# A decoder layer with routed experts: w_out's columns permuted in the split, the residual stored once, x's tile given to expert weights

## The chip, the cores and the metric

The kernel runs on one core of a Trainium2 chip. The metric is device time in microseconds (us), the median of three runs; lower is better.

## The reference, cut to what matters

```
h   = rms_norm(x, norm_attn)                       # x: 256 tokens x 1024
P   = h @ w_in                                     # queries, latent, dilated q/k/v, two gates
A   = latent attention;  Bd = dilated attention in three groups, merged
merged = sigmoid(gA) * (A @ w_o_mla) + sigmoid(gB) * (Bd @ w_o_dil)
x   = x + merged @ w_out                           # 1024 x 1024
h2  = rms_norm(x, norm_ffn)
gp  = softmax(h2 @ w_rg + b_rg); one of 4 groups per token
ep  = softmax of the 8 experts' logits of that group; the best two, renormalised
y   = sum over a token's experts of  weight * (silu(h2 @ w_gate[e]) * (h2 @ w_up[e])) @ w_down[e]
out = x + y                                        # 32 experts, d_ff 256
```

All tensors are f32. The experts' weights are 96 MiB of the 144 MB that are read from memory.

## The kernel before

Tokens stand in two blocks of 128 (tb 0 and 1), one token per partition. Every matmul of the first part (w_in to w_out) is done in three passes of a rounded format: each weight is split into a high part (ScalarE: a rounding copy, tile wh) and a low part (weight minus high part, tile wl, mostly on GpSimd in two operations of 128x512, now and then on VectorE), and each half unit, two blocks of 128 rows and 512 columns, takes 12 matmuls. wh and wl have three buffers each, so a split waits until TensorE has used the half unit three ahead of it. Raw weights come through four slots of 1 MiB (ring), loaded by SyncE's queue; a slot is loaded again when its last split has been read.

What order the instructions have is decided when the program is built, by a small simulator in the kernel (Weave) with prices for each engine; each engine then runs its queue in order.

w_out is the last matrix of the first part: Chunk objects outs[0] and outs[1] are its two column halves, and add_half lists eight half units. The last two are run block by block, each followed by x_out(tb, half): VectorE adds the residual in x1 to the accumulator and writes x1 back, and the squares are summed for the norm (ScalarE, for the last one VectorE). x_turn transposes the new x on TensorE for the router, logits multiplies by the router's weights, out_rms computes the reciprocal root in nine tiny steps (generator rms0 on GpSimd, rms1 on VectorE), and route picks groups and experts on VectorE; its two blocks' steps are interleaved. The experts' matmuls run on gathered tokens: gather multiplies tok (x with columns sorted by k of q*8 + k) by a one-hot matrix of 32 slots for each expert. x_sorted makes tok from x1, three times on GpSimd and once on ScalarE. warm_up issues matmuls without a use, to keep TensorE busy while VectorE routes.

The experts are done in eight groups g of four. Each group needs twelve loads of 1 MiB in order (four w_gate, four w_up, four w_down). All slots that the first part no longer needs (side, late_slot, oT, hT0, ring, and xs0 to xs3, which lie on the first part's buffers) become slots for expert weights: release(slot) puts a slot in the queue of free ones and pump issues the next loads of moe_loads on SyncE. There are 23 such slots with the four early ones, and a group's slots are given back after its gate, its up and its down matmuls. Group 0's gate slots (early) are loaded again in halves. In group 0 four matmuls with the identity put the residual x1 into the banks ys, to which combine adds each group's result. The last group's result is copied into x1 and stored.

Of the kernel before, what the change touches and what calls it, by code (L numbers as in the profile page):

```python
# [22 lines left out]
P = 128  # L23
# [36 lines left out]
TUNE = dict(gap=0.103, dV=0.05, dS=0.208, dG=0.121, dPE=0.257, early=-0.366, norm=0.02, split1=-0.463, split2=1.641, pace=2.246, small=9.132, masks=18.02, busy=6, first=40.0, space=0.0, busy2=0, busy3=4, rms=4.0, angles=3.0, keep=2, keep2=2, keep3=6, route=7, route2=6)  # L60
# [82 lines left out]
def layer(ctx, tc, A, out):  # L143
# [93 lines left out]
    with ExitStack() as c1:  # L237
# [42 lines left out]
        R_CKV, R_GQ, R_GK, R_MQ, R_MK, R_FFN = 0, 2, 5, 8, 9, 10  # L280
# [712 lines left out]
        def x_out(tb, half):  # L993

            xs, acc = x1[:, tb, half * 512:(half + 1) * 512], sso[:, tb, half:half + 1]
            V.scalar_tensor_tensor(xs, outs[half].acc[tb], 0.5, xs, op0=ALU.mult, op1=ALU.add)
            if tb and half:
                V.tensor_tensor_reduce(out=sqs[1], in0=xs, in1=xs, scale=1.0 / D, scalar=0.0, op0=ALU.mult, op1=ALU.add,
                                       accum_out=acc)
            else:  # L1000
                S.activation(sqs[0], xs, AF.Square, scale=D ** -0.5, accum_out=acc)

        def x_sorted(tb, half, E):
            src = x1[:, tb, half * 512:(half + 1) * 512].rearrange("p (q k) -> p k q", k=8)
            dst = tok[:, tb, :, half * 64:(half + 1) * 64]
            if E is S:
                S.activation(dst, src, AF.Copy)
            else:
                E.tensor_copy(dst, src)

        def x_turn(tb, half):
            for k in range(4):
                PE.transpose(pts[half][:, k], x1[:, tb, half * 512 + k * P:half * 512 + (k + 1) * P], ident)
            dst = xT[tb][:, 4 * half:4 * half + 4]
            S.copy(dst, pts[half])
# [76 lines left out]

        outs = [Chunk(A["w_out"][0], hTh, hTl, 8, 512, None, wait_merged(0)) for half in range(2)]
        out_u = {(k0, half): add_unit(outs[half].w, k0, 4, half * 512, 512) for k0 in (0, 4) for half in range(2)}
        for k0, q, half in ((0, 0, 0), (0, 2, 0), (0, 0, 1), (0, 2, 1), (4, 0, 0), (4, 0, 1), (4, 2, 0), (4, 2, 1)):
            add_half(outs[half], out_u[k0, half], q, 0, k0 + q)
# [17 lines left out]
        SP.dma_start(rows[R_FFN:R_FFN + 8], A["norm_ffn"].rearrange("o (k p) -> (o k) p", p=P))  # L1114
# [4 lines left out]
        def split_src(i):  # L1119
            hv = halves[i]  # L1120
            n = hv["c"].n
            return [hv["u"]["t"][:, hv["q"]:hv["q"] + 2, hv["col"]:hv["col"] + n]] + \
                [t[i % NSPLIT][:, :2 * n].rearrange("p (k n) -> p k n", k=2) for t in (whs, wls)]
# [207 lines left out]
        def router_weights():  # L1331
            yield 120.0
            SP.dma_start(rbias[:, NE:], bcast(A["b_router_group"], EG))
            SP.dma_start(rbias[:, :NE], bcast(A["b_router_expert"], NE))
            SP.dma_start(wr[:, :, NE:], A["w_router_group"].rearrange("o (k p) n -> p (o k) n", p=P))
            SP.dma_start(wr[:, :, :NE], A["w_router_expert"].rearrange("o (k p) n -> p (o k) n", p=P))
            SP.dma_start(g8, A["norm_ffn"].rearrange("o (q k) -> q (o k)", k=8))
            yield 30.0
            for k in range(8):
                G.tensor_scalar(wr[:, k], wr[:, k], cols[:, R_FFN + k:R_FFN + k + 1], None, op0=ALU.mult)  # L1340
                yield 2.0
# [10 lines left out]
        def half_unit(i, tbs=(0, 1)):  # L1352
# [15 lines left out]
            hi, lo, ready = split_of[i]  # L1368
            weave.ready, weave.last = ready, None
# [32 lines left out]
        for half in range(2):  # L1402
            x_sorted(0, half, G)
        half_unit(n_last + 1, (1,))
        x_out(1, 1)
        x_turn(1, 0)
        logits(0, 0)
        x_turn(1, 1)
        x_sorted(1, 0, G)
        x_sorted(1, 1, S)  # L1410
# [7 lines left out]
        rms1, r0, r1 = out_rms(1, V), route(0), route(1)  # L1418
# [27 lines left out]
    with ExitStack() as c2:  # L1446
# [136 lines left out]
        ov = out.rearrange("b (t p) d -> p (b t) d", p=P)  # L1583
        for g in range(NGRP):
# [43 lines left out]
            if g == 0:  # L1628
                for tb in range(2):
                    for half in range(2):  # L1630
                        PE.matmul(ys[2 * tb + half], ident, x1[:, tb, half * 512:(half + 1) * 512], start=True,
                                  stop=False, skip_group_check=True)

            def combine(piece):
# [3 lines left out]
                for tb in range(2):  # L1638
                    PE.matmul(yv[tb], trs[:, 2 + tb], dos[piece], start=False, stop=final, skip_group_check=True)
                if final:  # L1640
                    sl = slice(c0, c0 + n)
                    S.activation(x1[:, 0, sl], yv[0], AF.Copy)
                    V.tensor_copy(x1[:, 1, sl], yv[1])
                    nc.scalar.dma_start(ov[:, 0, sl], x1[:, 0, sl])
                    SP.dma_start(ov[:, 1, sl], x1[:, 1, sl])
# [54 lines left out]
```

## Time and profile before

| what | value |
|---|---|
| median of three runs | 514.99 us (514.86 to 515.1) |
| the profiled execution | 515.22 us |
| its span, first to last instruction | 513.4 us |
| TensorE busy | 463.3 us (90%) |
| GpSimd busy | 236.7 us (46%) |
| VectorE busy | 215.1 us (42%) |
| ScalarE busy | 170.2 us (33%) |
| read from memory | 144.00 MB |

The span is one execution as the hardware profiler recorded it; the time has 1.8 us more around it. In the profile's rows PE is TensorE, PEld its weight loads, DVE VectorE, ACT ScalarE, POOL GpSimd and SP SyncE; SPq is SyncE's queue of load commands. Almost every compute instruction has line L128, that of a recording helper, so rows are told apart by the names of tiles: x is x1, pj an accumulator, s and pt banks, gu, pd, px, tr and y the banks of the experts' part.

### The profile page before, as it was taken

How to read it: one execution, taken by the hardware profiler on the slowest of the kernel's cores; microseconds unless marked ns; L12 is line 12 of the kernel's file. 1: busy time of each engine (PE TensorE's matmuls, PEld its weight loads, DVE VectorE, ACT ScalarE, POOL GpSimd, SP SyncE). 2: the span in 40 equal slices, each digit the busy share in tenths (PEclk: the TensorE clock that was granted, in tenths of full speed). 3: DMA queues.
4: the chain of work that ended last, by engine and by line, in shares of the span. 5: the costliest groups of instructions: out<-in, count | busy, mean ns of one | idle time of the engine just before them, and what ended most of it. 6: DMA issues, size and time to landing. Idle time of an engine off the chain costs nothing.

```text
span 513.4 us, 8417 instructions
## 1 busy us (share of the span) xinstructions
PE 463.3 (90%) x3280; PEld 328.9 (64%) x3280; DVE 215.1 (42%) x516; ACT 170.2 (33%) x326; POOL 236.7 (46%) x266
## 2 busy tenths in 40 slices
PE   7939889998999999999999999997988878768997
PEld 4839668887778888888888886462535444325343
DVE  5985796648853430483344166122212130202002
ACT  4417546665654664475445330000000000000001
POOL 5828779786877889368698740000000000000000
PEclk9979999999999999999999999999999999988999
DMA  8653776655434545359896986999999999999992
GB/s 286 216 168 104 281 285 194 201 165 164 97 95 152 165 153 179 101 157 373 314 363 233 423 335 252 423 420 421 419 420 421 418 419 423 420 419 421 410 345 92
DMA packets 43956, 145.63 MB, mean 284 GB/s; under 512 B 5752, under 2 KB 11402, under 8 KB 33162
## 3 DMA queue, kind: packets, MB, share of 16 engines
q1 hardware_dynamic: 43194, 144.53, 74.6%
q8 instruction: 27, 0.44, 0.4%
q10 hardware_dynamic: 720, 0.53, 0.3%
q14 instruction: 15, 0.12, 0.1%
HBM read 144.00 MB, written 1.05 MB: 283 GB/s over the span
## 4 chain that ended last, share of the span: by engine, by line
PE 56%; DMA 26%; DVE 6%; POOL 6%; issue 4%; ACT 1%; SPq 0%; POOLq 0%; DVEq 0%; ACTq 0%
PE pj L128 36%; DMA xs<-in_w_up_dram 8%; PE pt L128 6%; DMA side<-in_w_gate_dram 4%; DMA side<-in_w_up_dram 4%; DMA oT<-in_w_down_dram 4%; PE gu L128 3%; POOL wl L128 3%; PE px L128 3%; PE s L128 3%; DMA ring<-in_w_down_dram 3%; PE y L128 3%; DMA early<-in_w_down_dram 2%; PE pd L128 2%; DMA ring<-in_w_in_dram 1%
## 5 line engine op out<-in xcount | busy, mean ns | idle before, releaser
L128 PE MATMUL pj<-wh,hT 128*128 128x512 f32 (+2 forms) x576 | 192.7, 397 | 3.3 <-DVE late_slot L128 1.8
L128 POOL TENSOR_TENSOR wl<-ring,wh 128x512 fp32r<-128x512 f32 (+2 forms) x130 | 162.7, 1276 | 53.3 <-ACT wh L128 52.7
L128 PEld LDWEIGHTS pj<-wh,hT 128*128 128x128 f32 x576 | 111.2, 195 | 24.0 <-ACT wh L128 3.8
L128 PE MATMUL pj<-wl,hT 128*128 128x512 f32 (+2 forms) x288 | 111.2, 386 | 0.7 <-DVE wl L128 0.7
L128 ACT ACTIVATE wh<-ring 128x1024 fp32r<-128x1024 f32 (+2 forms) x78 | 79.4, 1018 | 83.7 <-PE pj L128 66.1
L128 POOL TENSOR_TENSOR wc<-wc,comb 128x128 f32<-128x128 f32 x16 | 6.0, 399 | 171.1 <-DVE wc L128 171.1
L128 PEld LDWEIGHTS pj<-wl,hT 128*128 128x128 f32 x288 | 56.4, 196 | 8.1 <-DVE wl L128 0.9
L128 PE MATMUL gu<-side,xg 128*32 128x256 f32 x416 | 44.1, 401 | 5.4 <-DMA side<-in_w_up_dram 4.6
L128 ACT ACTIVATE he<-gu 128x256 f32<-128x256 f32 x8 | 3.1, 383 | 127.2 <-PE gu L128 127.2
L128 PE MATMUL y<-do,trs 128*128 128x512 f32 x56 | 27.8, 618 | 11.7 <-DVE do L128 6.6
L128 DVE SCALAR_TENSOR_TENSOR he<-he,gu 128x256 f32<-128x256 f32 x8 | 3.4, 421 | 82.6 <-ACT he L128 82.6
L128 POOL TENSOR_TENSOR side<-side,st 128x512 f32<-128x512 f32 (+2 forms) x32 | 30.8, 990 | 5.9 <-DVE st L128 5.9
L128 PEld LDWEIGHTS gu<-side,xg 128*32 128x32 f32 x416 | 21.1, 116 | 16.7 <-DMA side<-in_w_up_dram 6.5
L128 PEld LDWEIGHTS y<-do,trs 128*128 128x128 f32 x56 | 9.5, 189 | 31.1 <-DVE do L128 12.9
L128 DVE COPY do<-px 128x512 f32<-128x512 f32 x7 | 4.8, 691 | 50.3 <-PE px L128 50.3
L128 PE MATMUL gu<-ring,xg 128*32 128x256 f32 x176 | 25.7, 380 | 0.0
L128 DVE COPY side<-pt 128x512 f32<-128x512 f32 (+2 forms) x26 | 16.6, 645 | 17.4 <-PE pt L128 16.1
L128 DVE TENSOR_TENSOR wl<-ring,wh 128x1024 fp32r<-128x1024 f32 (+1 forms) x13 | 17.1, 1316 | 15.2 <-ACT wh L128 15.1
L128 PE MATMUL pt<-ident,late_slot 128*128 128x128 f32 (+1 forms) x84 | 13.2, 281 | 11.0 <-DVE cols L128 7.8
L128 ACT ACTIVATE do<-pd 128x512 f32<-128x512 f32 x7 | 4.2, 597 | 52.3 <-PE pd L128 52.3
L128 PE MATMUL pj<-wh,oT 128*128 128x512 f32 x64 | 21.1, 398 | 0.0
L128 PE MATMUL gu<-xs,xg 128*32 128x256 f32 x160 | 19.0, 381 | 2.1 <-DMA xs<-in_w_up_dram 2.1
(274 smaller groups left out, 753.7 us busy)
## 6 DMA issues: line engine op xcount, KB each, us to landing
ring<-in_w_in_dram SPq DMA_DIRECT2D x25, 1024.0 KB, 5.2
side<-in_w_up_dram SPq DMA_DIRECT2D x16, 1024.0 KB, 17.6
side<-in_w_gate_dram SPq DMA_DIRECT2D x10, 1024.0 KB, 18.5
early<-in_w_gate_dram SPq DMA_DIRECT2D x7, 1024.0 KB
side<-in_w_down_dram SPq DMA_DIRECT2D x6, 1024.0 KB, 5.0
ring<-in_w_gate_dram SPq DMA_DIRECT2D x6, 1024.0 KB, 17.0
xs<-in_w_up_dram SPq DMA_DIRECT2D x6, 1024.0 KB
xs<-in_w_down_dram SPq DMA_DIRECT2D x6, 1024.0 KB, 18.6
```

The source lines that it names most:

```text
L128: r = f(*args, **kw)
```

## The change

x_out now adds the residual and writes straight into tok, in the gathers' order. For that the accumulators must come in that order, so w_out's columns are permuted when its splits are made: split_src reads a slot as 8 columns apart ("p k (q r) -> p k r q"), and a unit is two row blocks of all 1024 columns in place of four of 512, since half r0 to r0+3 takes columns from everywhere. x_out reads x1 with the same step. x_sorted and its four calls go. x_turn reads tok, and the router's weights are loaded with rows in that order (and scaled by g8, a tile that was there already, so one small load of norm_ffn goes). x1 is released as a slot for expert weights after the last x_out: 24 slots. The residual enters the banks in group 2, read from tok with a step of 128, and group 0's combine starts them. The result is stored from tok. rms1 runs on GpSimd. In TUNE, route goes from 7 to 3 and route2 from 6 to 4 (the numbers of warm-up matmuls).

```diff
         def x_out(tb, half):
-            xs, acc = x1[:, tb, half * 512:(half + 1) * 512], sso[:, tb, half:half + 1]
-            V.scalar_tensor_tensor(xs, outs[half].acc[tb], 0.5, xs, op0=ALU.mult, op1=ALU.add)
+            rs = slice(4 * half, 4 * half + 4)
+            xs, acc = tok[:, tb, rs], sso[:, tb, half:half + 1]
+            V.scalar_tensor_tensor(xs, outs[half].acc[tb].rearrange("p (r q) -> p r q", r=4), 0.5,
+                                   x1[:, tb].rearrange("p (q r) -> p r q", r=8)[:, rs], op0=ALU.mult, op1=ALU.add)
+            xs = xs.rearrange("p r q -> p (r q)")
...
-        def x_sorted(tb, half, E):
-            src = x1[:, tb, half * 512:(half + 1) * 512].rearrange("p (q k) -> p k q", k=8)
-            dst = tok[:, tb, :, half * 64:(half + 1) * 64]
-            if E is S:
-                S.activation(dst, src, AF.Copy)
-            else:
-                E.tensor_copy(dst, src)
-
         def x_turn(tb, half):
             for k in range(4):
-                PE.transpose(pts[half][:, k], x1[:, tb, half * 512 + k * P:half * 512 + (k + 1) * P], ident)
+                PE.transpose(pts[half][:, k], tok[:, tb, 4 * half + k], ident)
...
-        out_u = {(k0, half): add_unit(outs[half].w, k0, 4, half * 512, 512) for k0 in (0, 4) for half in range(2)}
-        for k0, q, half in ((0, 0, 0), (0, 2, 0), (0, 0, 1), (0, 2, 1), (4, 0, 0), (4, 0, 1), (4, 2, 0), (4, 2, 1)):
-            add_half(outs[half], out_u[k0, half], q, 0, k0 + q)
+        out_u = [add_unit(outs[0].w, k0, 2, 0, D) for k0 in range(0, 8, 2)]
+        for i, half in ((0, 0), (1, 0), (0, 1), (1, 1), (2, 0), (2, 1), (3, 0), (3, 1)):
+            add_half(outs[half], out_u[i], 0, half, 2 * i)
...
-            return [hv["u"]["t"][:, hv["q"]:hv["q"] + 2, hv["col"]:hv["col"] + n]] + \
-                [t[i % NSPLIT][:, :2 * n].rearrange("p (k n) -> p k n", k=2) for t in (whs, wls)]
+            parts = [t[i % NSPLIT][:, :2 * n].rearrange("p (k n) -> p k n", k=2) for t in (whs, wls)]
+            if hv["c"] in outs:
+                r0 = 4 * hv["col"]
+                return [hv["u"]["t"].rearrange("p k (q r) -> p k r q", r=8)[:, :, r0:r0 + 4]] + \
+                    [t.rearrange("p k (r q) -> p k r q", r=4) for t in parts]
+            return [hv["u"]["t"][:, hv["q"]:hv["q"] + 2, hv["col"]:hv["col"] + n]] + parts
...
-        for half in range(2):
-            x_sorted(0, half, G)
         half_unit(n_last + 1, (1,))
         x_out(1, 1)
+        release(x1.rearrange("p t d -> p (t d)"))
         x_turn(1, 0)
         logits(0, 0)
         x_turn(1, 1)
-        x_sorted(1, 0, G)
-        x_sorted(1, 1, S)
...
-        rms1, r0, r1 = out_rms(1, V), route(0), route(1)
+        rms1, r0, r1 = out_rms(1, G), route(0), route(1)
...
-            if g == 0:
+            if g == 2:
                 for tb in range(2):
                     for half in range(2):
-                        PE.matmul(ys[2 * tb + half], ident, x1[:, tb, half * 512:(half + 1) * 512], start=True,
+                        PE.matmul(ys[2 * tb + half], ident,
+                                  tok[:, tb, :, half * 64:(half + 1) * 64].rearrange("p r q -> p q r"), start=False,
                                   stop=False, skip_group_check=True)
...
-                    PE.matmul(yv[tb], trs[:, 2 + tb], dos[piece], start=False, stop=final, skip_group_check=True)
+                    PE.matmul(yv[tb], trs[:, 2 + tb], dos[piece], start=g == 0, stop=final, skip_group_check=True)
```

Three places in the order of instructions. The first is SyncE's queue between the last loads into ring slots and the first half loads into group 0's gate slots (early); x_58 is x1's tile, xs_... the four slots on the first part's buffers.

```order
 L212 DMA ring_63<-in_w_up_dram 128x2048
-L212 DMA xs_2645<-in_w_up_dram 128x2048
-L212 DMA xs_2646<-in_w_down_dram 128x2048
-L212 DMA xs_2647<-in_w_down_dram 128x2048
-L212 DMA xs_2648<-in_w_down_dram 128x2048
-L228 DMA early_78<-in_w_down_dram 128x1024
+L212 DMA x_58<-in_w_up_dram 128x2048
+L212 DMA xs_2635<-in_w_down_dram 128x2048
+L212 DMA xs_2636<-in_w_down_dram 128x2048
+L212 DMA xs_2637<-in_w_down_dram 128x2048
+L212 DMA xs_2638<-in_w_down_dram 128x2048
+L228 DMA early_78<-in_w_gate_dram 128x1024
```

Five whole loads stand there in place of four, and group 0's gate slots take the next group's gate weights in place of one w_down and three w_gate. The second place is the end of GpSimd's queue in the first part, behind the splits and most of block 0's reciprocal root (rs_vo, rs_to and rstd are a root's tiles, sso the sums of squares); before:

```order
L128 TENSOR_SCALAR rs_to_2514<-rstd_149,rs_vo_2513 128x1
L128 TENSOR_SCALAR rstd_149<-rs_to_2514,rstd_149 128x1
L128 TENSOR_SCALAR rs_to_2514<-rstd_149,rs_vo_2513 128x1
L128 TENSOR_SCALAR rstd_149<-rs_to_2514,rstd_149 128x1
L128 COPY tok<-x_58 128x8x64 x3
```

and of the change:

```order
L128 TENSOR_SCALAR rstd_149<-rs_to_2513,rstd_149 128x1
L128 TENSOR_SCALAR rs_vo_2565<-sso 128x1
L128 TENSOR_SCALAR rstd_149<-rs_vo_2565 128x1
L128 TENSOR_SCALAR rs_vo_2565<-rs_vo_2565 128x1
L128 TENSOR_SCALAR rs_to_2566<-rstd_149,rs_vo_2565 128x1
```

The three copies are gone, and block 1's root (nine operations, the first four shown) follows block 0's. The third place is VectorE's queue from the x_outs on (the ISA rows are the last sum of squares; s_136 holds block 0's logits).

```order
-L128 SCALAR_TENSOR_TENSOR x_58<-pj,x_58 128x512 x4
-L128 ISA xg,sso<-x_58 128x512
+L128 SCALAR_TENSOR_TENSOR tok<-pj,x_58 128x512 x4
+L128 ISA xg,sso<-tok 128x512
 L128 ISA sso 128x1
-L128 TENSOR_SCALAR rs_vo_2571<-sso 128x1
-L128 TENSOR_SCALAR rstd_149<-rs_vo_2571 128x1
-L128 TENSOR_SCALAR rs_vo_2571<-rs_vo_2571 128x1
-L128 TENSOR_SCALAR rs_to_2572<-rstd_149,rs_vo_2571 128x1
-L128 TENSOR_SCALAR rstd_149<-rs_to_2572,rstd_149 128x1
-L128 TENSOR_SCALAR rs_to_2572<-rstd_149,rs_vo_2571 128x1
 L128 SCALAR_TENSOR_TENSOR el_lg<-s_136,rstd_149,rbias 128x36
```

The x_outs write tok, and block 1's root has left VectorE, where it stood before and between block 0's first routing steps.

## Rows read from the trace of the kernel before

**Rows 1.** The page: its first line, and the shares of the last chain by engine.

```profile
span 513.4 us, 8417 instructions
...
PE 56%; DMA 26%; DVE 6%; POOL 6%; issue 4%; ACT 1%; SPq 0%; POOLq 0%; DVEq 0%; ACTq 0%
```

**Rows 2.** The chain in order of time: start us, us, what; three pieces.

```profile
281.20 13.75 PE pj L128 x60
...
334.73 13.65 DMA ring<-in_w_down_dram
...
441.87 19.81 DMA side<-in_w_up_dram
```

**Rows 3.** Windows: busy us of PE, PEld, DVE, ACT, POOL; PE clock, DMA share, GB/s.

```profile
298.00:300.00 2.00, 2.00 (x18) 1.87 (x17) 1.33 (x3) 1.37 (x4) 1.65 (x4) 1.00 0.30 49
...
310.00:312.00 2.00, 2.00 (x30) 1.59 (x33) 1.52 (x4) 0.28 (x2) 0.00 (x0) 1.00 0.19 74
312.00:314.00 2.00, 2.00 (x45) 1.18 (x39) 1.32 (x8) 0.48 (x5) 0.00 (x0) 1.00 0.09 14
314.00:316.00 2.00, 2.00 (x44) 1.23 (x40) 1.79 (x8) 0.00 (x0) 0.00 (x0) 1.00 0.81 238
322.00:324.00 2.00, 2.00 (x16) 1.72 (x15) 0.90 (x3) 0.00 (x0) 0.00 (x0) 1.00 1.03 422
```

**Rows 4.** Timeline of SyncE's queue: start us, us, line, what is loaded.

```profile
298.62 0.33 SPq L212 DMA_DIRECT2D xs<-in_w_up_dram  x1
301.20 2.11 SPq L212 DMA_DIRECT2D xs<-in_w_down_dram  x3
312.88 0.33 SPq L228 DMA_DIRECT2D early<-in_w_down_dram  x1
```

**Rows 5.** Timeline, 294 to 311 us: x_outs, block 0's root, routing, gate.

```profile
294.98 0.69 DVE L128 SCALAR_TENSOR_TENSOR x<-pj,x 128x512 f32<-128x512 f32 x1 [0.67 <-PE pj L128]
...
296.58 0.31 POOL L128 TENSOR_SCALAR rs_vo<-sso 128x1 f32<-128x1 f32 x1 [3.29 <-ACT xg L128]
...
298.63 0.69 DVE L128 SCALAR_TENSOR_TENSOR x<-pj,x 128x512 f32<-128x512 f32 x1 [1.14 <-PE pj L128]
...
299.22 0.88 POOL L128 TENSOR_SCALAR rs_to<-rstd,rs_vo 128x1 f32<-128x1 f32 x1
...
300.20 0.26 POOL L128 TENSOR_SCALAR rstd<-rs_to,rstd 128x1 f32<-128x1 f32 x1
...
302.61 1.11 DVE L128 SCALAR_TENSOR_TENSOR el_lg<-pen,el_lg 128x32 f32<-128x32 f32 x1
...
303.65 0.24 DVE L128 SCALAR_TENSOR_TENSOR el_lg<-pj,rstd,rbias 128x36 f32<-128x36 f32 x1
...
310.94 3.66 PE L128 MATMUL gu<-early,xg 128*32 128x256 f32 x64
```

**Rows 6.** TensorE's waits, 424 to 465 us: us in total, times, longest.

```profile
PE gu L128 <- DMA side<-in_w_up_dram: 4.6, 3, 1.9
PE gu L128 <- DMA xs<-in_w_up_dram: 2.1, 2, 1.9
```

**Rows 7.** Timeline of TensorE: the residual matmuls in group 0.

```profile
323.34 3.60 PE L128 MATMUL y<-x,ident 128*128 128x512 f32 x8
```

**Rows 8.** Groups by form: busy us, mean ns of one, idle before.

```profile
L128 ACT ACTIVATE xg<-x 128x512 f32<-128x512 f32 x3 | 1.9, 634 | 5.0 <-DVE x L128 5.0
...
L128 ACT ACTIVATE tok<-x 128x512 f32<-128x512 f32 x1 | 1.1, 1144 | 0.0
...
L128 POOL COPY tok<-x 128x512 f32<-128x512 f32 x3 | 3.3, 1129 | 0.0
```

**Rows 9.** Timeline of GpSimd: the low parts of w_out's last split.

```profile
290.75 2.55 POOL L128 TENSOR_TENSOR wl<-ring,wh 128x512 fp32r<-128x512 f32 x2 [0.17 <-ACT wh L128]
```

**Rows 10.** Timeline of ScalarE: the high parts of w_out's second and last splits.

```profile
272.07 1.06 ACT L128 ACTIVATE wh<-ring 128x1024 fp32r<-128x1024 f32 x1 [0.18 <-PE pj L128]
...
289.61 1.06 ACT L128 ACTIVATE wh<-ring 128x1024 fp32r<-128x1024 f32 x1 [1.66 <-PE pj L128]
```

More of the change, by code (lines that the diff above doesn't have):

```diff
@@ L57, in split_const @@
     return parts
-TUNE = dict(gap=0.103, dV=0.05, dS=0.208, dG=0.121, dPE=0.257, early=-0.366, norm=0.02, split1=-0.463, split2=1.641, pace=2.246, small=9.132, masks=18.02, busy=6, first=40.0, space=0.0, busy2=0, busy3=4, rms=4.0, angles=3.0, keep=2, keep2=2, keep3=6, route=7, route2=6)
+TUNE = dict(gap=0.103, dV=0.05, dS=0.208, dG=0.121, dPE=0.257, early=-0.366, norm=0.02, split1=-0.463, split2=1.641, pace=2.246, small=9.132, masks=18.02, busy=6, first=40.0, space=0.0, busy2=0, busy3=4, rms=4.0, angles=3.0, keep=2, keep2=2, keep3=6, route=3, route2=4)
 class Weave:
@@ L277, in layer @@
         qn2 = sgB[:, 1].rearrange("p (t n) -> p t n", t=2)
-        R_CKV, R_GQ, R_GK, R_MQ, R_MK, R_FFN = 0, 2, 5, 8, 9, 10
+        R_CKV, R_GQ, R_GK, R_MQ, R_MK = 0, 2, 5, 8, 9
         at_once = iter(range(0, 2048, 64))
@@ L1113, in layer @@
         SP.dma_start(rows[R_MK:R_MK + 1, :QD], A["k_norm_mla"])
-        SP.dma_start(rows[R_FFN:R_FFN + 8], A["norm_ffn"].rearrange("o (k p) -> (o k) p", p=P))
         for i, name in enumerate(("q_norm_mla", "k_norm_mla")):
@@ L1334, in router_weights @@
             SP.dma_start(rbias[:, :NE], bcast(A["b_router_expert"], NE))
-            SP.dma_start(wr[:, :, NE:], A["w_router_group"].rearrange("o (k p) n -> p (o k) n", p=P))
-            SP.dma_start(wr[:, :, :NE], A["w_router_expert"].rearrange("o (k p) n -> p (o k) n", p=P))
+            SP.dma_start(wr[:, :, NE:], A["w_router_group"].rearrange("o (p k) n -> p (o k) n", p=P))
+            SP.dma_start(wr[:, :, :NE], A["w_router_expert"].rearrange("o (p k) n -> p (o k) n", p=P))
             SP.dma_start(g8, A["norm_ffn"].rearrange("o (q k) -> q (o k)", k=8))
@@ L1339, in router_weights @@
             for k in range(8):
-                G.tensor_scalar(wr[:, k], wr[:, k], cols[:, R_FFN + k:R_FFN + k + 1], None, op0=ALU.mult)
+                G.tensor_scalar(wr[:, k], wr[:, k], g8[:, k:k + 1], None, op0=ALU.mult)
                 yield 2.0
@@ L1368, in half_unit @@
             hi, lo, ready = split_of[i]
+            if c in outs:
+                hi, lo = (t.rearrange("p k r q -> p k (r q)") for t in (hi, lo))
             weave.ready, weave.last = ready, None
@@ L1583, in layer @@
         ov = out.rearrange("b (t p) d -> p (b t) d", p=P)
+        yo = tok.rearrange("p t r q -> p t (r q)")
         for g in range(NGRP):
@@ L1638, in combine @@
                 for tb in range(2):
-                    PE.matmul(yv[tb], trs[:, 2 + tb], dos[piece], start=False, stop=final, skip_group_check=True)
+                    PE.matmul(yv[tb], trs[:, 2 + tb], dos[piece], start=g == 0, stop=final, skip_group_check=True)
                 if final:
                     sl = slice(c0, c0 + n)
[L1642 to L1645, printed above, removed]
+                    S.activation(yo[:, 0, sl], yv[0], AF.Copy)
+                    V.tensor_copy(yo[:, 1, sl], yv[1])
+                    nc.scalar.dma_start(ov[:, 0, sl], yo[:, 0, sl])
+                    SP.dma_start(ov[:, 1, sl], yo[:, 1, sl])
             def down(i, piece):
```

## The prediction

> **What bounds the kernel now.** I read the page first. TensorE is busy for 90% of the span, but the chain that ended last gives it only 56% and transfers 26% [rows 1], so the kernel has stages with different limits. In order of time that chain belongs to transfers almost without a break from 334.73 to 441.87 + 19.81 = 461.68 us [rows 2], and the windows show why: 422 GB/s around 323 us [rows 3]. An expert load of 1 MiB takes 1.05 MB / 422 GB/s = 2.5 us, a group of twelve 30 us. From 315 us on the kernel is a stream of loads; what it ends at is when that stream starts running without holes, plus a tail that hangs on it. The reader is to look for the holes ahead of it. There are two: 49 GB/s in 298 to 300 us, and 74, 14 and 238 GB/s in the three windows from 310 to 316 us [rows 3]. SyncE's queue shows why. It issues one load into xs at 298.62 and three from 301.20, which are in by about 310.4, and then has no free slot until group 0 has done half of its gate matmuls: the halves into early start at 312.88 [rows 4], 1.94 us after the first gate matmul at 310.94 [rows 5], and the rate comes back about 2 us later. Does TensorE have room to follow an earlier stream? It waited 4.6 + 2.1 = 6.7 us for up weights between 424 and 465 us [rows 6], so up to that much of a gain gets through.
>
> **The extra slot.** x1 becomes free after the last x_out, and its 1 MiB load stands ahead of the xs loads. The fourth x_out ran from 298.63 to 299.32 [rows 5]; the x1 load can go out some 0.2 us later, against 298.62 for the first xs load now, so the first hole grows by about 0.9 us. The five loads then run from about 301.2 for 5 x 2.5 = 12.5 us, to 313.7, where four now end at 310.4. The second hole still ends when group 0's gate releases its slots, at the same time as now plus a change D of the routing. At that restart one load more is in: the stream is **2.5 - D us ahead**, the bigger first hole included, as long as the five are in before about 314.8. From there loads and groups are the same in number, with 24 slots for 23. Group 0 gives its down slots back earlier, since the residual matmuls (3.60 us [rows 7]) leave it, less what waits they cover, so no new hole opens near 334.
>
> **The routing, D.** The second token block's reciprocal root moves from VectorE to GpSimd, behind the first one's, and its first use is the biased logits of block 1, at 303.65 now [rows 5]. GpSimd's nine operations for block 0 run from 296.58 to 300.46 [rows 5]; the same again starts no sooner and would end near 304.2, 304.4 with the hand-over, so +0.7. One of the nine took 0.88 us; were it as short as the 0.31 of the first, it is +0.1. VectorE's queue holds block 0's rest and all of block 1's routing behind that wait, and TensorE the ranks, gathers and gate behind those. Against it: the masking of block 0 took 1.11 us at 302.61 [rows 5] while GpSimd copied tok; those three copies (1.129 us each) and ScalarE's are gone [rows 8]. Were the root early enough, the chain could gain at most that 1.11 us less the operation's own work and what TensorE needs for block 1's logits; I take half, -0.5, as the lower end. The warm-up matmuls, 7 in place of 13, only fill TensorE's waits for VectorE: 0. The x_outs now read x1 with a step of 8 elements. No row of VectorE has such a read; ScalarE's copy of that pattern took 1.144 us where its contiguous read of 512 takes 0.634 [rows 8], so 0 to 0.5 us on the last x_out, of which the root's wait hides most. I take D = +0.3, within -0.5 and +1.0.
>
> **The split of w_out, L.** This is the cost I trust least. Each of eight splits reads 1024 columns with that step: ScalarE once, GpSimd twice 512. ScalarE: 1.06 us becomes up to 1.06 + 2 x 0.51 = 2.08. The last split's ScalarE part starts at 289.61 [rows 10], when TensorE gives its buffer back, so it would end at 291.7, and GpSimd's 2.55 us [rows 9] at 294.35. Its last matmuls begin 0.46 us ahead of the x_out at 294.98 [rows 5], so they want it by 294.5: hidden, with 0.15 us to spare. GpSimd is the question. It spends 2 x 1.275 us [rows 9] on a split that TensorE takes 2.75 us to use (60 matmuls in 13.75 us [rows 2], twelve to a split). With p the new price of one operation, the second split can start near 275.3 (ScalarE's start at 272.07 [rows 10] is pushed to 273.1 by the longer first split, and it takes 2.08) and fourteen operations follow without a gap: L = 275.3 + 14p - 294.5, nothing below p = 1.37, 2.2 at 1.53, 5.7 at 1.275 + 0.51 = 1.785. The bounds are p = 1.275 (GpSimd's two streams share the time and the stepped one hides in it) and 1.785 (ScalarE's surcharge in full). The nearest row is GpSimd's copy of this very pattern, 1.129 us for 512 [rows 8], less than its two-operand 1.275, so the stepped stream alone is not slower than the pair of streams already is. For that reason I take p up to 1.37 and **L = 0** (to 0.5), and keep 5.7 as the far end.
>
> **Edits at nothing.** GpSimd's three copies of tok follow its roots at 300.46 and end by 303.9; the gathers that read them stand behind a one-hot that stands behind the logits at 303.65: off the path, as is ScalarE's. The residual in group 2 rather than group 0 reads tok with a step of 128; at ScalarE's surcharge of 1 ns an element its eight rows would cost 4.1 us more, and with the 2.2 us gained that is 6.3 of the 6.7 us that TensorE has over [rows 6]: covered, just. One small load fewer at the start, router weights with longer rows, and w_out units of 2 x 1024 columns (slots come back after splits 3, 4, 6, 8 for 2, 4, 7, 8) leave the queue full until 297 us as it is.
>
> **Sum.** -2.5 + 0.3 + 0 = -2.2 us. The profiled execution took 515.22 us (513.4 span and 1.8 around it), 0.2 over the median of 514.99, so I take the sum from the median: **512.8 us**.
>
> **The rivals.** (1) *GpSimd becomes the bound of the w_out stage*, which ends on the other side. It decides from p = 1.53: a surcharge of 0.26 us per operation, half of what ScalarE shows for the same pattern. At the whole of it the last x_outs, the x1 load and everything behind come 5.7 us later: 512.8 + 5.7 = 518.5 us. For it: ScalarE's pair of rows, and a GpSimd that is 93% busy there (2.55 of 2.75 us). Against it: the copy of 1.129 us. The Trainium skill, page "GPSIMD Engine Reference", section "Performance pitfalls for Q7 kernels", says that a read of SBUF whose step is over 8 bytes costs about 50% more per element. By that rule p would be 1.9, L 7.4 and the time about 520 us; no row here has a contiguous GpSimd copy of 512 beside the stepped one, so the trace does not show it either way. 33%. (2) *GpSimd pays a little*, p = 1.40 to 1.53: L of 0.4 to 2.2 eats the gain: 513.2 to 515. 15%. (3) *The extra slot brings nothing*: the five loads start so late that they end behind the restart, or TensorE can't follow because the stepped residual costs over 4.5 us. The wait of 6.7 us speaks against it. 515.2 us. 4%. (4) *The routing gets shorter*, D = -0.5, since GpSimd no longer copies beside it: 515.0 - 3.0 = 512.0. 8%. The forecast itself has 40%, with its own range of 512.2 to 513.7.
>
> **How the numbers follow.** A measurement of this kernel tells a change from none at about 0.2%, 1.03 us, so same is 513.96 to 516.02. Faster: the forecast, (4), and two fifths of (2): 54%. Same: the rest of (2), (3) and the lowest of (1): 14%. Slower: the rest of (1), 32%. For 8 in 10 the range starts at 512.0 (7% below, parts of (4)) and reaches into (1) up to 517.6 (p about 1.72), with some 12% above.
>
> **What would show it.** Right: the split operations on GpSimd stay under 1.37 us and ScalarE's near 2.08 or less; the x_out for the second half of block 0 starts within 0.5 us of 294.98; the x1 load goes out near 299.5; the rate stays at about 420 GB/s until about 313.7 and the low stretch ahead of the gate's releases shrinks from some 4 us to about 1; the biased logits of block 1 come near 303.9; TensorE's wait for up weights is still there, and the last load lands some 2 us earlier. Wrong: split operations of 1.55 us and over, ScalarE waiting on GpSimd for its buffers, TensorE waiting on wl in the last five splits; or a first hole that grows by several microseconds.

## The result and the profile after

The changed kernel takes **518.03 us** (median of 11, 516.24 to 520.33) against 514.99 us (11 runs): ratio 1.006, 95% interval 1.0044 to 1.0077. It is slower by 0.6%, where the prediction had 512.8 us, faster by 0.4%. The profiled execution took 516.24 us (span 514.4), the shortest of the eleven. Two executions, one of e16 (1591.89 us) and one of the kernel before in the set of e1 to e4 (1166.43 us), were in a slow state and are left out of the medians below.

Before the change does anything that counts, the two profiled executions are already 1.43 us apart: ScalarE's first split of w_out starts at 268.45 us before and at 267.02 after. That is no effect of the change: two experiments below with the change's instructions up to that point, e5 and e6, stand at 268.40 and 271.56. So below, times of different profiles are compared **from this split on**, as an absolute time less that start.

The timeline of the changed kernel, on the engines that the prediction spoke of (start us, us, engine, line, operation; in brackets the idle time before it and its releaser):

```profile
267.02 2.24 ACT L128 ACTIVATE wh<-ring 128x1024 fp32r<-128x1024 f32 x1 [1.72 <-PE pj L128]
...
269.35 3.38 POOL L128 TENSOR_TENSOR wl<-ring,wh 128x512 fp32r<-128x512 f32 x2 [0.91 <-ACT wh L128]
273.67 22.79 POOL L128 TENSOR_TENSOR wl<-ring,wh 128x512 fp32r<-128x512 f32 x14 [0.94 <-ACT wh L128]
...
297.29 1.16 DVE L128 SCALAR_TENSOR_TENSOR tok<-pj,x 128x512 f32<-128x512 f32 x1 [1.98 <-PE pj L128]
...
299.36 0.31 POOL L128 TENSOR_SCALAR rs_vo<-sso 128x1 f32<-128x1 f32 x1 [2.90 <-ACT xg L128]
...
300.94 1.08 DVE L128 SCALAR_TENSOR_TENSOR tok<-pj,x 128x512 f32<-128x512 f32 x1 [0.66 <-PE pj L128]
...
302.05 0.33 SPq L212 DMA_DIRECT2D x<-in_w_up_dram  x1
302.47 3.32 SPq L212 DMA_DIRECT2D xs<-in_w_down_dram  x4
...
303.34 0.29 POOL L128 TENSOR_SCALAR rs_vo<-sso 128x1 f32<-128x1 f32 x1
...
304.70 0.19 DVE L128 SCALAR_TENSOR_TENSOR el_lg<-pen,el_lg 128x32 f32<-128x32 f32 x1
...
306.38 0.27 POOL L128 TENSOR_SCALAR rstd<-rs_to,rstd 128x1 f32<-128x1 f32 x1
306.68 0.26 DVE L128 SCALAR_TENSOR_TENSOR el_lg<-pj,rstd,rbias 128x36 f32<-128x36 f32 x1 [1.79 <-POOL rstd L128]
...
309.38 1.13 PE L128 MATMUL pj<-wr,tok 128*128 128x128 f32 x8 [0.44 <-DVE sel L128]
...
313.68 3.66 PE L128 MATMUL gu<-early,xg 128*32 128x256 f32 x64
...
315.63 5.70 SPq L228 DMA_DIRECT2D early<-in_w_gate_dram  x8
...
369.75 7.07 PE L128 MATMUL y<-tok,ident 128*128 128x512 f32 x8
...
461.66 6.37 PE L128 MATMUL gu<-side,xg 128*32 128x256 f32 x58 [1.88 <-DMA side<-in_w_up_dram]
```

The reader is to see three things. GpSimd's fourteen low parts run without one gap, one every 22.79 / 14 = **1.628 us**, where [rows 9] has 2.55 / 2 = 1.275. ScalarE's high part takes 2.24 us against 1.06 [rows 10], but no wait of TensorE names it. The fourth x_out, 30.18 us after the first split in [rows 5], now comes 33.92 us after it: 3.74 us later. The routing and the restart behind it are later by as much or more: the halves into early, 44.43 us after the split in [rows 4], come at 48.61. TensorE's waits between 270 and 300 us name the engine, for its matmuls and for its weight loads (before has no such row):

```profile
PEld pj L128 <- POOL wl L128: 4.6, 6, 1.0
PE pj L128 <- POOL wl L128: 2.0, 6, 0.6
```

The windows of the changed kernel show the two holes again (columns as in [rows 3]):

```profile
300.00:302.00 2.00, 2.00 (x16) 1.77 (x14) 1.34 (x2) 1.62 (x4) 1.44 (x6) 1.00 0.28 119
302.00:304.00 2.00, 1.99 (x19) 1.90 (x19) 0.97 (x4) 0.64 (x2) 1.63 (x5) 1.00 0.43 74
304.00:306.00 2.00, 2.00 (x16) 1.88 (x16) 0.78 (x5) 0.00 (x0) 1.48 (x6) 1.00 1.02 430
306.00:308.00 2.00, 0.54 (x3) 0.13 (x2) 1.32 (x13) 0.00 (x0) 0.54 (x2) 1.00 0.98 406
...
314.00:316.00 2.00, 2.00 (x44) 1.22 (x40) 1.13 (x7) 0.77 (x5) 0.00 (x0) 1.00 0.97 401
316.00:318.00 2.00, 2.00 (x44) 1.16 (x36) 1.76 (x11) 0.00 (x0) 0.00 (x0) 1.00 0.70 207
318.00:320.00 2.00, 2.00 (x44) 1.20 (x40) 1.93 (x3) 0.00 (x0) 0.00 (x0) 1.00 0.77 172
```

The first hole (119 and 74 GB/s) is longer than in [rows 3], the second, which was 74 and 14 GB/s, is gone but for a slow refill at 207 and 172. So the slot does what was forecast of it. TensorE is busy for only 0.54 us of 306 to 308: it waits for the routing.

### The profile page after: what moved, and what is told of

It is laid out like the page before. It is cut to its first block, busy times and chain, and to the rows that moved or that the text cites. A ratio compares the mean times of both kernels' runs of the same rounds, so it can differ in the third digit from the quotient of the medians.

```text
span 514.4 us, 8410 instructions
## 1 busy us (share of the span) xinstructions
PE 466.6 (91%) x3274; PEld 328.8 (64%) x3274; DVE 214.6 (42%) x507; ACT 178.2 (35%) x325; POOL 241.9 (47%) x272
## 3 DMA queue, kind: packets, MB, share of 16 engines
HBM read 144.00 MB, written 1.05 MB: 282 GB/s over the span
## 5 line engine op out<-in xcount | busy, mean ns | idle before, releaser
L128 PE MATMUL pj<-wh,hT 128*128 128x512 f32 (+2 forms) x576 | 192.7, 398 | 2.8 <-DVE late_slot L128 1.8
L128 POOL TENSOR_TENSOR wl<-ring,wh 128x512 fp32r<-128x512 f32 (+2 forms) x130 | 168.6, 1334 | 50.5 <-ACT wh L128 50.1
L128 ACT ACTIVATE wh<-ring 128x1024 fp32r<-128x1024 f32 (+2 forms) x78 | 88.8, 1140 | 81.9 <-PE pj L128 63.7
L128 PEld LDWEIGHTS pj<-wl,hT 128*128 128x128 f32 x288 | 56.3, 195 | 12.6 <-POOL wl L128 4.6
L128 PE MATMUL gu<-side,xg 128*32 128x256 f32 x320 | 34.1, 420 | 4.0 <-DMA side<-in_w_up_dram 3.7
L128 PE MATMUL gu<-ring,xg 128*32 128x256 f32 x256 | 30.8, 380 | 0.0
L128 PEld LDWEIGHTS gu<-side,xg 128*32 128x32 f32 x320 | 16.3, 120 | 14.8 <-DMA side<-in_w_up_dram 5.0
L128 PEld LDWEIGHTS gu<-ring,xg 128*32 128x32 f32 x256 | 15.5, 110 | 11.9 <-issue 3.8
L128 DVE CUSTOM_DVE_ANT_0 side<-s,side 128x512 f32<-128x512 f32 (+2 forms) x32 | 15.4, 520 | 12.6 <-PE s L128 12.6
```

Source lines behind the costliest of these rows:

```text
L128: r = f(*args, **kw)
```

## The experiments

One table for all; each row's kernel is told below. All are timed in five rounds against the kernel before (514.7 to 515.1 us in every set). In e1, e5, e6, e9, e12 and e13 w_out's columns meet other columns of the residual, so these kernels don't compute the layer and stand for a time only. The five columns of times come from the one profiled execution of each, in us after ScalarE's first split of w_out: the fourth x_out, the first of the five whole loads, the first half load into early, the start of group 6's remaining up matmuls when the last up weights are in (461.66 in the timeline above), and the end of the span. Medians of two kernels whose intervals overlap are not told apart, and one profile is one execution.

| kernel | x_out 4 | first load | halves | group 6 | end | median us | ratio to before (95%) |
|---|---|---|---|---|---|---|---|
| before | 30.2 | 30.2 | 44.4 | 193.3 | 245.0 | 514.99 | |
| after | 33.9 | 35.0 | 48.6 | 194.6 | 247.4 | 518.03 | 1.0044 to 1.0077 |
| e1 plain splits | 30.2 | 31.3 | 46.9 | 192.9 | 244.6 | 515.00 | 0.9990 to 1.0029 |
| e2 low parts on VectorE | 31.4 | 32.5 | 47.5 | 193.9 | 245.4 | 515.62 | 1.0001 to 1.0039 |
| e3 root on VectorE | 33.9 | 35.0 | 47.3 | 194.2 | 247.1 | 516.58 | 1.0013 to 1.0063 |
| e4 the slot alone | 30.2 | 30.2 | 44.4 | 190.6 | 241.9 | 512.16 | 0.9936 to 0.9983 |
| e5 e1, root on VectorE | 30.3 | 31.4 | 43.7 | 190.9 | 243.8 | 514.03 | 0.9963 to 1.0008 |
| e6 e1, 18 warm-ups | 30.3 | 31.4 | 45.2 | 191.4 | 242.8 | 513.48 | 0.9949 to 0.9990 |
| e7 e2, root on VectorE | 31.4 | 32.5 | 44.9 | 192.7 | 244.9 | 515.33 | 0.9981 to 1.0020 |
| e8 e4, copies on ScalarE | 30.2 | 30.2 | 43.8 | 189.5 | 241.3 | 512.16 | 0.9927 to 0.9972 |
| e9 e4, stepped splits | 33.9 | 33.9 | 48.1 | 193.9 | 246.8 | 518.16 | 1.0022 to 1.0069 |
| e10 e4, root on GpSimd | 30.2 | 30.2 | 49.4 | 195.6 | 246.7 | 516.56 | 1.0015 to 1.0059 |
| e11 e4, 7 warm-ups | 30.2 | 30.2 | 45.2 | 191.1 | 244.0 | 514.27 | 0.9955 to 0.9999 |
| e12 e5, 13 warm-ups | 30.2 | 31.3 | 43.9 | 192.1 | 244.4 | 513.70 | 0.9969 to 1.0003 |
| e13 e12, x1 behind xs | 30.2 | 30.2 | 43.9 | 190.1 | 241.6 | 512.07 | 0.9929 to 0.9972 |
| e14 after, x1 behind xs | 33.9 | 33.9 | 50.0 | 196.0 | 247.7 | 517.94 | 1.0038 to 1.0077 |
| e15 after, 18 warm-ups | 33.9 | 35.0 | 48.9 | 195.0 | 247.5 | 517.15 | 1.0020 to 1.0062 |
| e16 e7, 13 warm-ups, x1 behind xs | 31.4 | 31.4 | 45.1 | 191.0 | 243.8 | 514.12 | 0.9970 to 1.0025 |

**The split: e1, e2, e9.** e1 is the change with plain reads in the splits, e2 moves the stepped low parts to VectorE:

```diff
-                return [hv["u"]["t"].rearrange("p k (q r) -> p k r q", r=8)[:, :, r0:r0 + 4]] + \
+                return [hv["u"]["t"].rearrange("p k (r q) -> p k r q", r=8)[:, :, r0:r0 + 4]] + \
```

> The changed kernel, but the splits of w_out read their columns side by side (so the columns that meet the residual are other ones and the output is not the layer's); all else stays. Theory A (the stepped read makes GpSimd the bound of the w_out stage, 1.63 us an operation for 1.28, and every x_out, the x1 load and the gate come some 3.6 us later): operations back at 1.28 us, x_outs without GpSimd waits, and about 3.6 us off the changed kernel's 518.0: 514.4, or a little less where the low clock in group 6 goes too. Theory B (the expert stream is what got worse: the slot, the slow refill of the gate slots, the residual with a step in group 2): at most 1 us off, above 517.

```diff
-            split_lo(i, V if late else G)
+            split_lo(i, V if late or halves[i]["c"] in outs else G)
```

> The changed kernel, with the low parts of w_out's eight splits on VectorE, which is nearly idle there (one operation of 128x1024, 1.3 us with a plain read, perhaps 2.2 with the step, against 2.75 us of TensorE's use). Theory A: GpSimd's bound is gone, so about the time of the plain split, 514.4. Theory B: above 517.

e1 measured 515.0 us, 3.0 less than the change, with the fourth x_out back at 30.2. e2 takes the load off GpSimd and leaves the step: 515.6 us. VectorE does the low part in 2.1 to 2.25 us for 1024 columns and is late by 1.25 us only, and ScalarE's longer high part, which is in e2 too, costs no more than that. e9 puts the step, and nothing else of the change's costs, into e4:

```diff
+            if hv["c"] in outs:
+                parts = [parts[0].rearrange("p k (q r) -> p k r q", r=8)] + \
+                    [t.rearrange("p k (r q) -> p k r q", r=8) for t in parts[1:]]
```

> The kernel before with the extra slot (512.2 us), and w_out's splits reading their columns 8 apart (so they meet the wrong columns of the residual): the price of the step by itself. Theory (GpSimd's operation of 1.63 us makes it the bound of that stage, L = 3.0 to 3.6 us): 515.2 to 515.8 us, x_outs and the gate some 3 us later. Rival (the load order and units of the change are what makes the splits late, not the step): 512.5 or less, with GpSimd's operation still at 1.6 us.

Its timeline, GpSimd's low parts and the second and fourth x_outs:

```profile
276.74 22.80 POOL L128 TENSOR_TENSOR wl<-ring,wh 128x512 fp32r<-128x512 f32 x14 [0.90 <-ACT wh L128]
...
300.37 0.69 DVE L128 SCALAR_TENSOR_TENSOR x<-pj,x 128x512 f32<-128x512 f32 x1 [2.38 <-PE pj L128]
...
304.04 0.69 DVE L128 SCALAR_TENSOR_TENSOR x<-pj,x 128x512 f32<-128x512 f32 x1 [1.14 <-PE pj L128]
```

The same 1.63 us per operation and the same 3.7 us on the fourth x_out as in the change, with the load order and the units of the kernel before: it is the step. Its time missed the expectation by 2.4 us: it is 6.0 us over e4 by the medians (5.0 by the means), more than the 3.7. In the profiles group 6 starts 3.3 us later, and from there to the end e9 takes 1.5 us longer, of which more below.

The medians also say that the costs don't add. Without the step the rest of the change costs 2.8 us (e1 against e4); with it, nothing that can be told (the change against e9: 518.03 and 518.16, with overlapping intervals). The place of the x1 load, below, shows the same.

**The slot: e4.** The kernel before, with the reordering copies as they were, x1's place lent to the loads behind the xs slots, residual and output through tok:

```diff
-        release(*extra_slots)
+        release(*extra_slots, x1.rearrange("p t d -> p (t d)"))
...
-            if g == 0:
+            if g == 2:
```

> The kernel before with the extra slot alone: tok is made by the copies as before, x1 is released behind the four xs slots, the residual is read from tok in group 2 and the output stored from tok. Theory A: the fifth load fills the hole ahead of the gate's releases, 2.5 us less than the kernel before: 512.5. Theory B: the slot gives nothing or costs something: 515 or above.

512.16 us, 0.4% under the kernel before and faster than both kernels of this study. The queue of SyncE, and the windows at the second hole:

```profile
298.57 0.33 SPq L212 DMA_DIRECT2D xs<-in_w_up_dram  x1
301.15 2.11 SPq L212 DMA_DIRECT2D xs<-in_w_down_dram  x3
303.65 0.33 SPq L212 DMA_DIRECT2D x<-in_w_down_dram  x1
312.83 5.77 SPq L228 DMA_DIRECT2D early<-in_w_gate_dram  x8
```

```profile
310.00:312.00 2.00, 2.00 (x32) 1.54 (x33) 1.49 (x4) 0.33 (x3) 0.00 (x0) 1.00 1.01 426
312.00:314.00 2.00, 2.00 (x44) 1.23 (x40) 1.36 (x8) 0.43 (x4) 0.00 (x0) 1.00 0.52 180
```

Nothing is later than before, five loads go out in place of four, 426 GB/s stands where [rows 3] has 74, and group 6 starts 2.7 us earlier.

**The root: e3, e5, e10.** One word, in three surroundings:

```diff
-        rms1, r0, r1 = out_rms(1, G), route(0), route(1)
+        rms1, r0, r1 = out_rms(1, V), route(0), route(1)
```

> The changed kernel, with block 1's reciprocal root back on VectorE. In the changed kernel the biased logits of block 1 waited 1.79 us for that root on GpSimd. Theory A says that the gate starts earlier by what the root gains, some 1.3 us: 516.7. If that wait stood beside another one that ends as late (the logits on TensorE), the time stays at 518.0.

> The change with w_out's columns read side by side by the splits (so they meet the wrong columns of the residual) and with block 1's reciprocal root back on VectorE. Theory: after the split, the root on GpSimd is the second cost; taking both away leaves the slot's gain less the dearer x_outs: 512.5 to 513.2 us, the gathers at about 1.05 us and no low clock around 304 to 312 us. Rival (the low clock comes from the fewer warm-up matmuls alone): 515, with the low clock still there. Rival (the rest is the stepped x_outs): 514.5, without a low clock, and the biased logits of block 1 within 0.3 us of where they stood with the root on GpSimd.

> The kernel before with the extra slot (512.2 us), and block 1's reciprocal root on GpSimd; 13 warm-up matmuls stay. Theory: the biased logits of block 1 come 0.7 to 1.4 us later and the time is 512.9 to 513.6. Rival (the root alone costs nothing, only together with the fewer warm-up matmuls, through the clock): 512.2, with the logits late all the same.

With the root on VectorE the halves come 1.3 us earlier in e3 (1.45 us in time against the change) and 3.2 us earlier in e5 than in e1 (1.0 us in time); the intervals overlap both times. Of the 3.2 us 1.9 are the gathers, which ran at the low clock in e1 (below) and not in e5. e5 stayed 0.8 us over its expectation all the same. e10, the other way round from e4, missed its expectation by 3 us: 516.56. There GpSimd still has the three copies of tok, 3.27 us, between the roots, and VectorE and TensorE wait for all of it:

```profile
300.15 3.27 POOL L128 COPY tok<-x 128x512 f32<-128x512 f32 x3
303.52 0.30 POOL L128 TENSOR_SCALAR rs_vo<-sso 128x1 f32<-128x1 f32 x1
...
306.88 0.26 DVE L128 SCALAR_TENSOR_TENSOR el_lg<-pj,rstd,rbias 128x36 f32<-128x36 f32 x1 [3.41 <-POOL rstd L128]
```

TensorE's clock stands at 0.50 from 308 to 310 us besides. So e10 doesn't price the root of the change, which has no copies ahead of it.

**The warm-up matmuls: e6, e11, e15.** They are matmuls of ones that fill TensorE's waits in the routing: 13 before, 7 after. e6 and e15 raise the count, e11 lowers that of e4 from 7 + 6 to 3 + 4:

```diff
-TUNE = dict(... route=3, route2=4)
+TUNE = dict(... route=7, route2=11)
```

> The change with w_out's columns read side by side by the splits, the root left on GpSimd, and more warm-up matmuls in the routing: 18 in place of 7 (before had 13). Theory (TensorE idles while it waits for GpSimd's root, its clock falls, and the gathers take 1.9 us in place of 1.05): the clock stays up, the gathers take about 1.05 us, and the time is 513.2 us. Rival (the clock falls for another reason, or the added matmuls stand in the way of the routing's own): 515 or more. The root's wait of about 1.7 us stays in both.

> The kernel before with the extra slot (512.2 us), and 7 warm-up matmuls in the routing in place of 13; root on VectorE. Theory (the fills matter only where TensorE waits long for the root): 512.2 and no low clock between 300 and 312 us. Rival (the fills alone hold the clock up): low clock there, gathers 1.9 us for eight in place of 1.05, 513.5 or more.

> The change whole, with 18 warm-up matmuls in the routing in place of 7. Theory (seven leave TensorE idle and in part of the executions its clock falls through the gathers): 516.5 us and no execution with the gathers at 2 us. Rival (in the whole change the clock stays up anyway, as in its profiled execution, where eight gathers took 1.13 us): 518.0.

In e1 TensorE waits for the root, busy for 0.61 us of 2, and then its clock stands at the lower of its two levels, 1.2 GHz (0.50), through the gathers; eight of these take 1.91 us in place of 1.05:

```profile
304.00:306.00 2.00, 0.61 (x4) 0.29 (x2) 1.47 (x13) 0.00 (x0) 0.38 (x2) 0.77 0.99 410
306.00:308.00 2.00, 2.00 (x7) 1.56 (x7) 1.30 (x8) 0.00 (x0) 0.00 (x0) 0.50 1.04 438
308.00:310.00 2.00, 2.00 (x12) 2.00 (x11) 0.41 (x2) 0.00 (x0) 0.00 (x0) 0.50 0.98 414
```

The eight gathers, in e1 and then in e6:

```profile
307.37 1.91 PE L128 MATMUL pj<-wr,tok 128*128 128x128 f32 x8
...
310.57 1.05 PE L128 MATMUL pj<-wr,tok 128*128 128x128 f32 x8
```

e6 adds eleven matmuls: the clock stays at 1.00, and 513.48 us is 1.5 less than e1, as the first theory had it. e11 takes six away from e4, with the root on VectorE, and the clock falls as the rival had it. TensorE waited 0.91 us there, and its eight gathers take 2.04 us. The median is 514.27 us, 2.1 over e4, but the intervals overlap, and in the profiles group 6 starts only 0.5 us later; the other 1.6 are lost in the tail. Its windows:

```profile
304.00:306.00 2.00, 1.09 (x4) 0.90 (x4) 1.97 (x18) 0.00 (x0) 0.00 (x0) 0.80 0.96 393
306.00:308.00 2.00, 2.00 (x9) 1.53 (x8) 0.60 (x4) 0.00 (x0) 0.00 (x0) 0.50 1.04 430
```

Where the clock doesn't fall, more matmuls bring nothing clear: e12 is e5 with six more, e5's gathers ran at 1.00 already, and e12 is 0.3 us faster. In the whole change (e15) eighteen matmuls bring 0.9 us, which the intervals don't tell from nothing. In the one profiled execution of the change the gathers took 1.13 us, though TensorE waited 1.46 us ahead of them, so there was little to bring back there. e14, with the same routing and 7 matmuls, shows that it can happen: granted clocks of 0.59 and 0.56 from 312 to 316 us and halves 1.4 us later than in the change.

**The place of the x1 load: e12, e13, e14.** In the change x1 is released ahead of the xs slots, so the first load waits for the last x_out; in e4 it goes last. e12 is e5 with the 13 matmuls; e13 is e12 with this, and e14 the change with it:

```diff
-        release(x1.rearrange("p t d -> p (t d)"))
...
-        release(*extra_slots)
+        release(*extra_slots, x1.rearrange("p t d -> p (t d)"))
```

> The change with plain splits (columns side by side, meeting the wrong residual columns), the root on VectorE and the 13 warm-up matmuls of before: of the change's costs only the stepped x_outs and the place of the x1 load ahead of xs are left. Theory (these leave the restart of the loads where it is): 512.2 to 512.8 us. Rival (the five loads that start 1.2 us later cost that, or the clock falls longer in the tail): 513.5 to 514, as without the matmuls.

> Plain splits, the root on VectorE, 13 warm-up matmuls (513.7 us so far), and the x1 slot handed to the loads behind the four xs slots in place of ahead of them, as in the kernel before with the extra slot. Theory (the first of the five loads goes out 1.2 us later when it must wait for the last x_out, and that is what is left between 513.7 and 512.2): first load at the time of before, 512.2 to 512.7 us. Rival (the first hole is covered by the restart, the rest is a longer low clock in the tail for another reason): 513.7.

> The change whole, with the x1 slot handed out behind the four xs slots. Theory: the first load leaves 1.2 us earlier, 516.8 us. Rival (with the splits late the restart is later too, and the five loads end before it anyway): 518.0.

e12 missed: 513.7, as its rival had it. e13 measured 512.07 us and is e4 again: by the medians the place of that load cost 1.6 us, of which the later start is 1.1; the intervals just overlap. SyncE's queue in e12:

```profile
298.34 0.33 SPq L212 DMA_DIRECT2D x<-in_w_up_dram  x1
298.76 3.33 SPq L212 DMA_DIRECT2D xs<-in_w_down_dram  x4
310.94 5.58 SPq L228 DMA_DIRECT2D early<-in_w_gate_dram  x8
```

From 298.34 to 310.94 are 12.6 us, just the 12.5 that five loads take: no time is left over, so the late start of the five has nothing to hide behind. In the change there are 13.58 us (302.05 to 315.63), 1.1 more than they take, so an earlier start brings nothing: e14, 517.94, as its rival had it.

**Together, and beyond: e7, e8, e16.** e7 is e2 with the root on VectorE, e16 is e7 with 13 matmuls and x1 behind xs. e8 is e4 with all four copies of tok on ScalarE:

```diff
-        for half in range(2):
-            x_sorted(0, half, G)
...
-        x_sorted(1, 0, G)
-        x_sorted(1, 1, S)
+        for tb in range(2):
+            for half in range(2):
+                x_sorted(tb, half, S)
```

> The change with w_out's low parts and block 1's reciprocal root both on VectorE. Theory: GpSimd holds up neither the splits nor the routing, what is left of the costs is the stepped x_outs: 513 to 514.2 us. Rival (VectorE at 2.1 to 2.25 us for a low part is late for TensorE too, or its queue delays the x_outs): 515.6, as with the low parts alone on VectorE.

> The change with each of its costs taken away where that can be done and the computation kept: w_out's low parts and block 1's root on VectorE, 13 warm-up matmuls, x1 behind xs. Theory: 512.5 to 513.3 us. Rival (VectorE's stepped low parts of 2.1 us, or a low clock in the tail, keep it back): 515, as with the low parts and the root on VectorE alone (515.3).

> The kernel before with the extra slot (which measured 512.2 us), and with all four reordering copies of tok on ScalarE. Theory (the masking of block 0 took 1.11 us because GpSimd copied beside it): it takes 0.3 us, the biased logits of block 1 come up to 0.9 us earlier, and the time is 511.3. Rival (block 1's root on VectorE ends last anyway, or the gathers wait for ScalarE's copies): 512.2 or a little over.

e7 stayed at 515.3, its rival. e16 came to 514.12, between its two values and no faster than before (0.9998); its low parts on VectorE and its x_outs still read with the step. Its group 6 starts within 0.4 us of e4's; the 1.5 us between them are lost after that, in the tail. e8's masking of block 0, 1.11 us in [rows 5], takes 0.19 us without the copies beside it, and its halves come 0.7 us earlier, but the median is e4's to the hundredth, its rival:

```profile
302.58 0.19 DVE L128 SCALAR_TENSOR_TENSOR el_lg<-pen,el_lg 128x32 f32<-128x32 f32 x1
```

**The tail.** From group 6's start to the end of the span the profiles of these kernels take between 51.1 and 52.9 us, with the same work. In every profile TensorE waits 1.4 to 1.9 us for the last up weights just ahead of that start, and how much of the matmuls behind the wait runs at the low clock differs. The 7 us from that start on, in before, e4, e9 and the change (columns as in [rows 3]):

```profile
461.73:468.73 7.00, 7.00 (x73) 4.19 (x74) 0.84 (x2) 0.38 (x1) 0.00 (x0) 0.75 1.01 420
...
458.99:465.99 7.00, 7.00 (x77) 4.42 (x78) 0.84 (x2) 0.38 (x1) 0.00 (x0) 0.80 1.01 421
...
464.07:471.07 7.00, 7.00 (x63) 3.44 (x64) 0.06 (x1) 0.38 (x1) 0.00 (x0) 0.59 1.02 424
...
461.66:468.66 7.00, 7.00 (x64) 3.44 (x65) 0.18 (x1) 0.38 (x1) 0.00 (x0) 0.60 1.02 425
```

Their tails are 51.7, 51.3, 52.8 and 52.7 us. Over the eighteen profiles a clock of 0.58 to 0.63 in these 7 us goes with a tail of 52.6 to 52.9 us, 0.67 and 0.69 with 52.3 and 52.2, and 0.75 to 1.00 with 51.1 to 51.7. So the tail follows that clock, and the 1.1 us more in the change and the 1.5 us between e9 and e4 go with it. Which clock an execution gets does not follow from the edits: e14, which differs from the change only in the place of the x1 load, has 0.76. No kernel here changes that clock by itself, so a correlation is shown and not a cause, and neither is it shown that the change has the longer tail in every execution. The executions of one kernel differ in the same way: of the change's eleven, the seven with a mean granted clock of 0.983 take 517.4 us on average, the three with 0.980 518.9, and the one with 0.977 520.3.

## Why the prediction was wrong

**The step that failed: "The split of w_out, L".** It took p, the price of one GpSimd operation, up to 1.37 us and L = 0. Measured p is 1.628, and by the step's own formula L = 275.3 + 14 x 1.628 - 294.5 = 3.6 us; the fourth x_out came 3.74 later in the change and 3.71 in e9. The formula and the place were right, the choice of p was not. With L = 3.6 the prediction's own sum comes to 516.4 us. The reason given was that GpSimd's copy of the pattern (1.129 us) is shorter than its two-operand operation (1.275), so the stepped stream would hide in the pair. It doesn't hide: the step adds 0.35 us on top. A one-operand row gives no bound for a two-operand operation from below. This is the mechanism of the first rival, at two thirds of its far end. The Trainium skill, page "GPSIMD Engine Reference", section "Performance pitfalls for Q7 kernels", has about one cycle more per element for a step over 8 bytes, and calls that 50%. The trace agrees that the step costs; an estimate with 50% of the whole operation made it 1.9 us, and the trace has 1.628, which is 28%.

**A second step, the fixed tail.** The prediction has "a tail that hangs on" the stream of loads, lets it move with the stream at an unchanged length, and gives no reason. In the profiles it grew from 51.7 to 52.7 us, with TensorE's clock at 0.60 in place of 0.75 behind group 6's last wait. The measured 518.03 lies 1.6 us over the 516.4, and this is 1.1 of it as far as the two profiles tell; why the clock was lower stays open.

**"The extra slot": right.** 2.5 us forecast; e4 measured 2.5 to 2.8 by the medians and 2.7 by group 6's start. The first hole grew by 1.1 us beyond the splits' delay, against 0.9 forecast. What the step said of it, that it is no loss as long as the five loads are in before the restart, fits e12 and e14.

**"The routing, D": right in size, in part by luck, and wrong in one term.** From the fourth x_out to the biased logits of block 1 it is 5.02 us before and 5.74 after: +0.72, the +0.7 of the text. But two things cancel in it, one that the text held to be hidden and one that it had only as an alternative. The x_outs with a step take 1.08 to 1.18 us in place of 0.69. For the first and the third the extra is hidden in the wait for TensorE ahead of the next, and the fourth's stands ahead of the x1 load. The second's is not hidden: block 0's root starts 2.07 us after that x_out (299.36 less 297.29) in place of 1.60 [rows 5], and block 1's root stands behind it. That root then takes 3.3 us (303.34 to 306.65) and not another 3.9, since the operation of 0.9 us does not come again. At the first gate matmul, 42.49 us after the first split before and 46.66 after, D is 46.66 - 42.49 - 3.74 = 0.43, against +0.3. The warm-up matmuls, costed at 0 because they only fill waits, are the wrong term: they can keep the clock up, and are worth 1.5 us in e1 (e6); in e4 (e11) and the change (e15) the medians have 2.1 and 0.9, not clear of noise. The gain of half the masking's 1.11 us was there too (0.19 us after), and it went into the root's wait of 1.79.

**"Edits at nothing": right.** The residual with a step took 7.07 us against 3.60 [rows 7], both at a clock of 1.00: +3.5, where 4.1 was worked out. e4 has it too, 7.07 us, and gains all the same.

**The account.** In the profiles group 6 starts 1.4 us later than before: -2.7 for the slot (e4), +3.3 for the step (e9 against e4), +0.4 for D, and 0.4 not accounted for. The tail adds 1.1, together 2.4 at the end of the span. The medians differ by 3.0; the profiled execution is the shortest of the eleven, and no profile shows the remaining 0.6. A low clock in the gathers, as in e14, is a candidate that is not shown.

## What to carry to other kernels

Before a copy is folded into another pass by a permuted read, price the permuted read on each engine that will make it, as a surcharge on the operation that it makes now and not as a bound from a shorter one; an engine that was 93% busy in a stage has no room for 28% more. A matmul that only fills a wait may not be free to take out: in e1 what stood behind the wait ran at half the clock. And a gain at one end is worth what the next meeting point leaves of it: the same earlier load came with 1.6 us by the medians where the five loads fill the gap, and with nothing where they leave 1.1 us before the restart.

## What the runs showed of the hardware

A read with a step cost on every engine that made it: of 32 bytes on the first three, of 512 on TensorE. GpSimd, two operands, one with the step, 512 columns: 1.275 to 1.628 us. ScalarE, 1024 columns: 1.06 to 2.24 us. VectorE, two operands, 512 columns: 0.69 to 1.08 to 1.18. TensorE, eight rows of 512 moving columns of float32, at a clock of 1.00: 3.60 to 7.07 us. GpSimd pays least for a column and was still the one that broke, being the one without room. The Trainium skill, page "SBUF — State Buffer", section "Door 1: The DMA port swizzle", says that each access which crosses to a new line of 16 bytes pays a penalty; the trace agrees on all four that the step costs, with these surcharges, and no run here varies the step to show the line.

The masking of 128x32 on VectorE took 1.11 us beside GpSimd's copies and 0.19 us without them (e8, and the change). When the gate slots are filled again by eight half loads, issued over 5.70 us in the change, the rate is 207 and 172 GB/s for 4 us, where it was 401 just before; whether the half loads or the spacing of their issues is the reason, no run shows.
